# Moving adaLN sums between stages and reordering the splits behind three boundaries in a two-layer fp32 trunk

## The chip, the cores and the metric

The kernel runs on one core of one Trainium2 chip. The metric is the device time of one execution in microseconds (us), as the median of the timed runs. Five engines of the core matter here: TensorE (PE, matmuls and transposes; PEld is its loading of weights, which overlaps), VectorE (DVE), ScalarE (ACT), GpSimd (POOL) and SyncE (SP). Each works through its own queue of instructions in order and waits on semaphores for the others. In this kernel SP's queue issues nearly all loads, POOL's queue issues a few loads and on-chip moves.

## The reference

Two layers over 512 tokens of width 1024, in fp32. Layer 0 mixes tokens by stick-breaking attention with 16 heads, layer 1 by a gMLP. Each mixer is followed by a SwiGLU of inner width 2816. Every sub-layer has a norm ahead of it and one behind it, and shift, scale and gate are computed from a vector c ("adaLN").

```python
def reference(x, c, ...):
    for i in range(DEPTH):
        shift, scale, gate = ada_modulation(c, mix_ada_w[i], mix_ada_b[i])
        h = rms_norm(x, mix_pre_g[i]) * (1.0 + scale) + shift
        if i % N_MIXERS == 0:
            y = stick_breaking_mixer(h, sb_w_qkv[j], sb_w_o[j])
        else:
            y = token_mixing_mixer(h, ...)
        x = x + gate * rms_norm(y, mix_post_g[i])
        shift, scale, gate = ada_modulation(c, ffn_ada_w[i], ffn_ada_b[i])
        h = rms_norm(x, ffn_pre_g[i]) * (1.0 + scale) + shift
        y = swiglu(h, ffn_w_gate[i], ffn_w_up[i], ffn_w_down[i])
        x = x + gate * rms_norm(y, ffn_post_g[i])
    return x
```

`ada_modulation` is `silu(c) @ w + b` with w of 1024 x 3072: 4 of these in all, 12 parts of 1024 x 1024 that have to be read and summed.

## The kernel before

**Tiling.** The 512 tokens are 4 tiles of 128 (tt = 0 to 3, in reversed order). Between stages the hidden state h stands transposed, as hT. TensorE multiplies in fp32r, and full precision comes from three products of high and low parts: `split` (L107) makes the high part by a copy on ScalarE and the low part by a subtraction on DVE, `mm3` (L99) issues high x high, high x low and low x high. So each weight, each hT and each activation costs one ScalarE and one DVE instruction. In rows of the profile the ends h and l tell the parts (wh, wl, hTh, hTl, Sh, Sl).

**Who orders the work.** Where `pe["chain"]` and the `chain` of the recorders `dve` and `act` (class `Written`, L55) are on, instructions run in the order of the program text; `order` (L80) adds a dependency that orders only and waits for nothing. Where the chains are off (v's stage, the boundaries, the FFNs and the gMLP) a scheduler places the instructions of each engine.

**Stages.** In the profiled execution v's stage runs to about 92 us, attention to 231, its output projection and first boundary to 280, the first FFN to 606, the boundary behind it to 638, the gMLP to 766, its boundary to 793, and the second FFN to the end.

**adaLN in the background.** `Bg` (L310) computes parts of the modulation (G a gate, A a scale, B a shift) in small steps. A step is one load of 512 KB (`rawada`, two buffers, the next load issued when one is free; in attention on POOL's queue) and one DVE `scalar_tensor_tensor` that adds it to an accumulator; eight steps make a part. Then the accumulator is split (`acch`, `accl`), and two matmuls against a matrix of ones sum it over the partitions (bank `adaps`). `bg.step(n)` is called wherever the code places it.

**v's stage and attention.** While q, k of pair 0 and the first half of v exist, the loop of L941 to L950 multiplies the second half of v over 8 k-blocks, and takes one adaLN step in each of the first six (L949). `evac_q` (L755) makes q on ScalarE and `qlow` on DVE, out of the bank `pqk`, and thus frees that bank; `evac_k` (L768) does it for k. Then 8 pairs of heads follow (L961). Each pair has seven places where `rest()` takes matmuls of the next pair's q and k (`FILLS`, L809) and adaLN steps (`SUMS`, L812, one row a pair). `scores` (L859) makes sigmoids `ga` on ScalarE and a scan over them on DVE. `v_next` (L827) makes V's differences along the tokens, for which it moves V by one row with five moves on POOL's queue, into two buffers, and `step_v` subtracts; the first half's is made at L936, the second's behind pair 0, with the subtractions behind pairs 1 and 2 (L983 to L986).

**Boundaries.** `out_proj` (L484) ends the mixers and the first FFN, and `boundary` (L407) goes with each tile: two squares and a root give the norm of y, then x is updated (x<-t,r,x), t is x times A, divided by x's own norm, plus B (t<-t,r,B), and TensorE transposes t in two banks (`tp`, L438), which `split` turns into hT. Tiles 0 and 1 keep copies `c`. Behind the boundaries of tiles 2 and 3, `sums` (L452) makes the four sums S that the block products need, split too. Boundaries 0 and 1 stand between matmuls of the projection. Ahead of those of tiles 2 and 3 a unit of the next stage is put (`nxt[0]`, `nxt[1]`, L548), which reads tiles 0 and 1 alone, and a third one behind (`nxt[2]`, L551). For the FFNs these are `Ffn.first` (L1038): units on bank `gu` over the first 256 tokens, with their weights made by `wget` two units ahead (`look`); for the gMLP `u_first` (L1284), on bank `u`.

**The FFN's blocks.** After three units over the other 256 tokens the FFN goes on in `seven` (L1041): a product of 2x2 blocks by seven products in place of eight (bank `r`), the third of which is the first to read a sum S. `blocks` (L168) prepares its weights from two loads, `rawx` and `rawy`: split of x, split `b21` (named b in the profile), the addition `f13` and two more (named f), and their splits.

**Weights.** `wemit` (L132) takes a weight from one of two raw buffers and splits it, in the order of the list `stream`. The look-ahead decides how early its split is issued.

Of the kernel before, what the change touches and what calls it, by code (L numbers as in the profile page):

```python
# [25 lines left out]
def trunk(ctx: ExitStack, tc: tile.TileContext, A: dict, out: bass.AP):  # L26
# [28 lines left out]
    class Written:  # L55

        def __init__(self, engine):
            self.engine, self.prev, self.chain = engine, None, False

        def __getattr__(self, name):  # L60
            f = getattr(self.engine, name)

            def call(*a, **k):
                b = f(*a, **k)  # L64
                if self.chain and self.prev is not None:
                    order(b, self.prev)
                self.prev = b
                return b

            return call  # L70
# [97 lines left out]
    def blocks(xr, yr):  # L168

        fp = fwork["pool"]  # L170
        x = wtile(KD, P)
        split(x[0][:], x[1][:], xr[:])
        b21 = [fp.tile([P, 4, P], F32R, tag=f"b21{i}", name=nm("b21")) for i in range(2)]
        split(b21[0][:], b21[1][:], yr[:, 0:4, :])
        f13 = fp.tile([P, KD, P], F32, tag="f13", name=nm("f13"))
        dve.tensor_tensor(
            f13[:].rearrange("p (a k) f -> p a (k f)", a=2),
            xr[:].rearrange("p (a k) f -> p a (k f)", a=2),
            yr[:, 4:8, :].rearrange("p (a k) f -> p a (k f)", a=1).to_broadcast([P, 2, 512]),
            ALU.add,  # L180
        )
        t13 = wtile(KD, P)
        split(t13[0][:], t13[1][:], f13[:])
        f24 = fp.tile([P, KD, P], F32, tag="f24", bufs=1, name=nm("f24"))
        dve.tensor_tensor(f24[:, 0:4, :], f13[:, 0:4, :], xr[:, 4:8, :], ALU.add)
        dve.tensor_tensor(f24[:, 4:8, :], f24[:, 0:4, :], yr[:, 0:4, :], ALU.add)
        t24 = wtile(KD, P)
        split(t24[0][:], t24[1][:], f24[:])

        def half(t, i):  # L190
            return lambda k: (t[0][:, 4 * i + k, :], t[1][:, 4 * i + k, :])

        return {
            "B11": half(x, 0), "B22": half(x, 1), "B21": half(b21, 0),
            "T1": half(t13, 0), "T3": half(t13, 1), "T2": half(t24, 0), "T4": half(t24, 1),
        }
# [210 lines left out]
    def boundary(s, tt, y, xin, hT, S, tag):  # L407

        halves = [slice(0, 512), slice(512, D)]
        sq = [small.tile([P, 1], F32, tag=f"sq{hf}", name=nm("sq")) for hf in range(2)]  # L410
        t = npool.tile([P, D], F32, tag="n", name=nm("t"))
        for hf, c in enumerate(halves):
            act.activation(junk[:, c], y[hf][:], AF.Square, accum_out=sq[hf][:])
            if hf == 1:
                sd, r2 = rms(sq[1][:], sq[0][:])
            dve.tensor_tensor(t[:, c], y[hf][:], ada["G", s][:, c], ALU.mult)
        dve.reciprocal(r2[:], sd[:])
        x = xin(tt)
        if s == 3:
            for c in halves:  # L420
                dve.scalar_tensor_tensor(x[:, c], t[:, c], r2[:, 0:1], x[:, c], ALU.mult, ALU.add)
                load(out[tt * P : (tt + 1) * P, c], x[:, c])
            return
        dve.scalar_tensor_tensor(x[:], t[:], r2[:, 0:1], x[:], ALU.mult, ALU.add)
        xd[tt] = dram.tile([P, D], F32, tag=f"x{tt}", bufs=2, name=nm("xd"))
        nc.gpsimd.dma_start(out=xd[tt][:], in_=x)
        sx = small.tile([P, 1], F32, tag="sx", name=nm("sx"))
        act.activation(junk[:], x[:], AF.Square, accum_out=sx[:])
        sd, r1 = rms(sx[:])
        dve.tensor_tensor(t[:], x[:], ada["A", s], ALU.mult)  # L430
        dve.reciprocal(r1[:], sd[:])
        dve.scalar_tensor_tensor(t[:], t[:], r1[:, 0:1], ada["B", s], ALU.mult, ALU.add)
        late = []
        for q in range(2):
            ps = bank("tp", tag)
            for k in range(4):
                kk = q * 4 + k
                transpose(ps[:, k * P : (k + 1) * P], t[:, kk * P : (kk + 1) * P])  # L438
            a = ps[:].rearrange("p (a b) -> p a b", a=4)
            if tt % 2 == 0:  # L440
                hT[tt // 2, q] = (slot(F32R, "hTh", 4, 256), slot(F32R, "hTl", 4, 256))
            c = slice(tt % 2 * P, (tt % 2 + 1) * P)
            th, tl = hT[tt // 2, q]
            split(th[:, :, c], tl[:, :, c], a)
            if S is not None and tt < 2:
                if tt == 0:
                    S["c", q] = slot(F32, "c", 4, 256)
                act.activation(S["c", q][:, :, tt * P : (tt + 1) * P], a, AF.Copy)
            late.append(a)
        return lambda: sums(S, tt, late)  # L450

    def sums(S, tt, a):  # L452

# [19 lines left out]
        part("3", f[:, 0])  # L473

    xd = {}

    def x_load(tt):

# [5 lines left out]
    def out_proj(s, nk, get_act, wkey, J, bg, hT, nxt=(), pre=None, S=None, steps=0, bg2=None):  # L484
# [61 lines left out]
        for n, tt in enumerate((2, 3)):  # L546
            if nxt:
                evacs.append(nxt[n]())  # L548
            late.append(boundary(s, tt, y[tt], xin, hT, S, "p" if tt == 3 else "b"))
        if nxt:  # L550
            evacs.append(nxt[2]())  # L551
            with tc.issue_after(last_sqrt[0].ins):
                for f in evacs:
                    f()
        if hT is not None:
            for f in late:
                f()

    def sqrt_table():
        with tc.issue_after(last_act[0].ins):  # L560
# [185 lines left out]
    with tc.tile_pool(name="att", bufs=1) as att, tc.tile_pool(name="att2", bufs=6) as att2:  # L746
# [62 lines left out]
        FILLS = ((2, 3, 2, 3, 2, 3, 1),) * 5 + (  # L809
            (2, 2, 2, 2, 2, 2, 0), (4, 2, 1, 1, 0, 0, 0), (3, 0, 2, 0, 2, 1, 0),  # L810
        )
        SUMS = ((1, 0, 1, 0, 1, 0, 0),) * 6 + ((1, 1, 1, 1, 1, 1, 0), (1, 0, 1, 0, 1, 1, 0))  # L812
        fgen = filler()

        def fill(n):
# [125 lines left out]
        for k in range(KD):  # L941
            if k % 2 == 0:
                wv = wget(("wv", 1, k // 2))
            v_step(vb, 1, k, wv)
            if k in (1, 4):
                cur[0](B31 if k == 1 else B2)
            if k >= 6:
                step_v(k - 6)
            if k < 6:  # L949
                bg.step(1)  # L950
        v_evac(vb, 1)
        tw = [bank("tw") for _ in range(2)]
# [8 lines left out]
        for i in range(NPAIR):  # L961
            scores, flip, values, finish = cur
            more = i + 1 < NPAIR
            if more:
                cur = attend(i + 1)
            F = iter(zip(FILLS[i], SUMS[i]))

            def rest():
                n, sums = next(F)
                fill(n)  # L970
                bg.step(sums)

            for group, js in zip((LATE, *EARLY), (B31, B2, B0)):
                flip(group, 0)
                flip(group, 1)
                rest()
                if more:
                    cur[0](js)
                rest()
            values()  # L980
            finish()
            rest()
            if i == 0:  # L983
                step_v = v_next(1)
            if i in (1, 2):
                step_v(i - 1)  # L986
        for _ in fgen:
            bg.step(1)
        bg.step(99)
# [16 lines left out]
    class Ffn:  # L1006
# [29 lines left out]
            return evac  # L1036

        def first(self):  # L1038
            return [lambda f=f: self.unit(f, 0, 256, 2) for f in range(NH)]

        def seven(self, f):  # L1041

# [456 lines left out]
```

## Time and profile before

| | us |
|---|---|
| median of 3 runs | 1132.68 (1132.51 to 1133.71) |
| the profiled execution | 1135.05 |
| its span on the core | 1133.3 |
| DVE busy | 893.4 (79%) |
| ScalarE busy | 597.7 (53%) |
| loading of weights into TensorE | 993.3 (88%) |
| mean DMA traffic | 155 GB/s |

The span is the stretch from the first to the last instruction in the trace, the execution's time has what lies around it too. A share of busy time is an average over stages that have different limits, so what a wait costs is read from the stage in which it stands. TensorE's granted clock is at 0.9 or more of full speed in every fortieth of the span.

In rows of the timeline the columns are: start in us, duration in us, engine, line, operation, output<-inputs, partitions x elements and type, and the number of instructions (x2: two of them in one row, with their joint duration); in brackets the idle time of that engine just before, and what ended it.

### The profile page before, as it was taken

What the parts mean: (1) busy time and instruction counts of PE and PEld (TensorE: products, weight loads), DVE (VectorE), ACT (ScalarE), POOL (GpSimd) and SP (SyncE); (2) the same over time, 40 slices, a digit from 0 to 9 for tenths busy, and PEclk for the clock granted to TensorE, in tenths of its full rate; (3) what the DMA queues carried; (4) which work ended last, traced back from release to release, by engine and by line L of the source; (5) the groups of instructions that cost most, each with busy time, mean ns of one, the idle gap of its engine ahead of it and who ended that gap; (6) DMA issues with size and microseconds to landing.
All of it is one profiled execution on the core that took longest, in us unless ns stands there. A gap on an engine that the chain in (4) does not pass through costs nothing.

```text
span 1133.3 us, 18148 instructions
## 1 busy us (share of the span) xinstructions
PE 1110.5 (98%) x7264; PEld 993.3 (88%) x7264; DVE 893.4 (79%) x1141; ACT 597.7 (53%) x971; POOL 39.8 (4%) x71
## 2 busy tenths in 40 slices
PE   7999999999999999999999999999999999999997
PEld 5787878778999999988878978988999999999895
DVE  7767988759988989687677765659988888788964
ACT  7745666646555555562334534437455555566541
POOL 0212010000000000010000000000000000000000
PEclk9999999999999999999999999999999999999999
DMA  9676444353244444378874572333244344223242
GB/s 363 224 221 186 149 149 132 129 186 132 92 131 150 143 134 133 95 229 262 286 262 151 195 268 83 106 130 131 84 140 140 124 134 144 75 78 109 93 167 75
DMA packets 51298, 176.09 MB, mean 155 GB/s; under 512 B 5643, under 2 KB 6155, under 8 KB 50318
## 3 DMA queue, kind: packets, MB, share of 16 engines
q1 hardware_dynamic: 45166, 153.95, 41.2%
q0 software_dynamic: 6048, 20.98, 6.0%
q8 instruction: 57, 0.93, 0.3%
q14 instruction: 27, 0.22, 0.1%
HBM read 164.43 MB, written 8.39 MB: 152 GB/s over the span
## 4 chain that ended last, share of the span: by engine, by line
PE 74%; DMA 12%; DVE 9%; issue 2%; ACT 2%; SPq 0%; DVEq 0%; ACTq 0%
PE r L88 32%; PE y L88 10%; PE X L88 8%; DMA rawada<-in_ada 6%; PE pqk L88 6%; PE gu L88 4%; PE v L88 3%; PE M L88 2%; DVE wl L64 2%; PE u L88 2%; PE z L88 2%; PE tw L96 1%; PE av L88 1%; DMA raw<-in_wdown 1%; DMA ada<-in_ada0w 1%
## 5 line engine op out<-in xcount | busy, mean ns | idle before, releaser
L64 ACT ACTIVATE wh<-raw 128x1024 fp32r<-128x1024 f32 (+1 forms) x112 | 117.1, 1051 | 142.1 <-PE y L88 36.3
L64 DVE TENSOR_TENSOR wl<-raw,wh 128x1024 fp32r<-128x1024 f32 (+1 forms) x112 | 135.1, 1211 | 63.4 <-ACT wh L64 62.9
L88 PE MATMUL r<-Sh,wh 128*128 128x256 f32 x608 | 170.6, 281 | 0.0
L88 PE MATMUL r<-Sl,wh 128*128 128x256 f32 x608 | 170.5, 280 | 0.0
L88 PE MATMUL r<-Sh,wl 128*128 128x256 f32 x608 | 170.3, 280 | 0.0
L88 PE MATMUL y<-wh,as 128*128 128x512 f32 x480 | 153.6, 396 | 0.6 <-DVE G L64 0.6
L64 DVE TENSOR_TENSOR wl<-f,wh 128x1024 fp32r<-128x1024 f32 x76 | 92.9, 1222 | 37.1 <-ACT wh L64 37.0
L64 ACT ACTIVATE wh<-f 128x1024 fp32r<-128x1024 f32 x76 | 80.6, 1061 | 75.1 <-PE r L88 65.1
L88 PEld LDWEIGHTS r<-Sh,wh 128*128 128x128 f32 x608 | 114.8, 189 | 0.2 <-ACT e L64 0.2
L88 PEld LDWEIGHTS r<-Sh,wl 128*128 128x128 f32 x608 | 114.8, 189 | 0.0
L88 PEld LDWEIGHTS r<-Sl,wh 128*128 128x128 f32 x608 | 114.7, 189 | 0.0
L88 PEld LDWEIGHTS y<-wh,as 128*128 128x128 f32 x480 | 90.1, 188 | 21.6 <-DVE G L64 1.1
L88 PE MATMUL y<-wl,as 128*128 128x512 f32 x240 | 94.7, 395 | 0.0
L88 PE MATMUL r<-hTh,wh 128*128 128x256 f32 x304 | 88.9, 293 | 0.1
L88 PE MATMUL r<-hTl,wh 128*128 128x256 f32 x304 | 85.1, 280 | 0.0
L88 PE MATMUL X<-wh,as 128*128 128x512 f32 (+1 forms) x288 | 84.7, 370 | 0.0
L88 PE MATMUL r<-hTh,wl 128*128 128x256 f32 x304 | 80.3, 280 | 0.0
L64 ACT ACTIVATE e<-r 128x256 f32<-128x256 f32 x114 | 43.5, 381 | 53.6 <-PE r L88 53.3
L88 PEld LDWEIGHTS r<-hTh,wh 128*128 128x128 f32 x304 | 57.2, 188 | 4.8 <-DVE gu L64 1.3
L88 PEld LDWEIGHTS X<-wh,as 128*128 128x128 f32 x288 | 52.5, 188 | 9.6
L88 PE MATMUL r<-hTh,b 128*128 128x256 f32 x304 | 60.8, 282 | 0.0
L64 ACT ACTIVATE wh<-rawx 128x1024 fp32r<-128x1024 f32 x38 | 40.3, 1061 | 34.0 <-PE r L88 31.0
(233 smaller groups left out, 2812.9 us busy)
## 6 DMA issues: line engine op xcount, KB each, us to landing
rawada<-in_ada SPq DMA_DIRECT2D x56, 512.0 KB, 4.7
raw<-in_wdown SPq DMA_DIRECT2D x44, 512.0 KB, 4.0
rawy<-in_wy SPq DMA_DIRECT2D x38, 512.0 KB, 3.6
rawx<-in_wx SPq DMA_DIRECT2D x38, 512.0 KB, 4.3
rawada<-in_ada POOLq DMA_DIRECT2D x24, 512.0 KB, 4.3
raw<-in_wqk SPq DMA_DIRECT2D x16, 512.0 KB, 4.2
ada<-in_ada0w SPq DMA_DIRECT2D x7, 1026.0 KB, 11.0
raw<-in_wgu SPq DMA_DIRECT2D x12, 512.0 KB, 3.6
```

Of the source, the lines that this page charges most:

```text
L64: b = f(*a, **k)
L88: b = nc.tensor.matmul(o, l, r, start=start, stop=stop, skip_group_check=True)
L96: last_tp[0] = nc.tensor.transpose(o, i, ident)
```

## The change

It has three parts.

1. **Boundaries.** `Written` gets a `gate`: while it is set, each recorded instruction is ordered behind that one. `boundary` no longer splits tile 2's transposes; that code is now the function `turned`, and `out_proj` calls it for tile 2 behind the boundary of tile 3, with DVE gated by tile 3's t (`ready[0]`) and ScalarE by its last root. The third unit, with its two weights and whatever its look-ahead makes, is called inside the gates too. The addition `f13` of every block is ordered behind `ready[0]`, and `first` gives the second unit no look-ahead, so that the third unit's weights are made where it stands itself.
2. **Sums.** v's stage takes four adaLN steps instead of six, and pairs five and six of attention take four each instead of three.
3. **V's second moves** are written behind pair 1 instead of pair 0, and their subtractions behind pairs 2 and 3.

```diff
@@ class Written @@
-            self.engine, self.prev, self.chain = engine, None, False
+            self.engine, self.prev, self.chain, self.gate = engine, None, False, None
...
+                if self.gate is not None:
+                    order(b, self.gate)
@@ def blocks @@
-        dve.tensor_tensor(
+        add = dve.tensor_tensor(
             f13[:].rearrange("p (a k) f -> p a (k f)", a=2),
...
+        order(add, ready[0])
@@ def boundary @@
-        dve.scalar_tensor_tensor(t[:], t[:], r1[:, 0:1], ada["B", s], ALU.mult, ALU.add)
+        ready[0] = dve.scalar_tensor_tensor(t[:], t[:], r1[:, 0:1], ada["B", s], ALU.mult, ALU.add)
...
-            a = ps[:].rearrange("p (a b) -> p a b", a=4)
-            if tt % 2 == 0:
+            late.append(ps[:].rearrange("p (a b) -> p a b", a=4))
+        if tt != 2:
+            turned(tt, hT, S, late)
+        return lambda: sums(S, tt, late), lambda: turned(tt, hT, S, late)
+
+    def turned(tt, hT, S, late):
+
+        for q, a in enumerate(late):
+            if (tt // 2, q) not in hT:
                 hT[tt // 2, q] = (slot(F32R, "hTh", 4, 256), slot(F32R, "hTl", 4, 256))
...
-            late.append(a)
-        return lambda: sums(S, tt, late)
...
+    ready = [None]
@@ def out_proj @@
         if nxt:
+            dve.gate, act.gate = ready[0], last_sqrt[0]
+            late[0][1]()
             evacs.append(nxt[2]())
+            dve.gate = act.gate = None
...
-                f()
+                f[0]()
@@ attention @@
-        SUMS = ((1, 0, 1, 0, 1, 0, 0),) * 6 + ((1, 1, 1, 1, 1, 1, 0), (1, 0, 1, 0, 1, 1, 0))
+        SUMS = ((1, 0, 1, 0, 1, 0, 0),) * 4 + ((1, 1, 1, 0, 1, 0, 0),) * 2 + ((1, 1, 1, 1, 1, 1, 0), (1, 0, 1, 0, 1, 1, 0))
...
-            if k < 6:
+            if k < 4:
                 bg.step(1)
...
-            if i == 0:
+            if i == 1:
                 step_v = v_next(1)
-            if i in (1, 2):
-                step_v(i - 1)
+            if i in (2, 3):
+                step_v(i - 2)
@@ Ffn.first @@
-            return [lambda f=f: self.unit(f, 0, 256, 2) for f in range(NH)]
+            return [lambda f=f: self.unit(f, 0, 256, 2 if f != 1 else 0) for f in range(NH)]
```

Numbers behind names in the rows below count tiles and differ between the two kernels. DVE's queue at the end of v's stage before (G<-rawada is an adaLN sum, wl a weight's low part, ga the scans, qlow what frees the bank pqk):

```order
L64 SCALAR_TENSOR_TENSOR G_568<-rawada_622,sc,G_568 128x1024
L64 SCALAR_TENSOR_TENSOR G_568<-rawada_637,sc,G_568 128x1024
L64 SCALAR_TENSOR_TENSOR G_568<-rawada_667,sc,G_568 128x1024
L64 TENSOR_TENSOR wl_731<-raw_726,wh_730 128x1024
L64 SCALAR_TENSOR_TENSOR ga_756<-ga_756,tri 128x512 x2
L64 SCALAR_TENSOR_TENSOR qlow<-pqk_725,q_767 64x512 x2
```

The same place in the changed kernel:

```order
L64 SCALAR_TENSOR_TENSOR G_568<-rawada_622,sc,G_568 128x1024
L64 TENSOR_TENSOR wl_725<-raw_720,wh_724 128x1024
L64 SCALAR_TENSOR_TENSOR ga_750<-ga_750,tri 128x512 x2
L64 SCALAR_TENSOR_TENSOR qlow<-pqk_719,q_761 64x512 x2
L64 TENSOR_TENSOR wl_772<-raw_722,wh_771 128x1024
```

Two sums no longer stand ahead of wl, the scans and qlow. DVE's queue in the second half of the sixth pair, before:

```order
L64 SCALAR_TENSOR_TENSOR qlow<-pqk_1616,q_1688 64x512 x2
L64 TENSOR_TENSOR wl_1709<-raw_1617,wh_1708 128x1024
L64 SCALAR_TENSOR_TENSOR B_1396<-rawada_1666,sc,B_1396 128x1024
L64 SCALAR_TENSOR_TENSOR ga_1725<-ga_1725,tri 128x256 x2
L64 SCALAR_TENSOR_TENSOR B_1396<-rawada_1718,sc,B_1396 128x1024
L64 SCALAR_TENSOR_TENSOR ga_1759<-ga_1759,tri 128x512 x2
L64 TENSOR_TENSOR k_1770<-pqk_1705,k_1770 64x512 x2
```

In the changed kernel:

```order
L64 SCALAR_TENSOR_TENSOR qlow<-pqk_1613,q_1685 64x512 x2
L64 SCALAR_TENSOR_TENSOR B_1496<-rawada_1663,sc,B_1496 128x1024
L64 TENSOR_TENSOR wl_1709<-raw_1614,wh_1708 128x1024
L64 SCALAR_TENSOR_TENSOR B_1496<-rawada_1692,sc,B_1496 128x1024
L64 SCALAR_TENSOR_TENSOR ga_1725<-ga_1725,tri 128x256 x2
L64 SCALAR_TENSOR_TENSOR B_1496<-rawada_1718,sc,B_1496 128x1024
L64 SCALAR_TENSOR_TENSOR ga_1759<-ga_1759,tri 128x512 x2
L64 TENSOR_TENSOR k_1770<-pqk_1705,k_1770 64x512 x2
```

One sum more stands there, between qlow and wl, and it works through its own load. DVE's queue at the boundary of tile 3 behind attention, before (t_2474 is tile 3's, hTl_2399 and hTl_2408 from tp_2393 and tp_2402 are tile 2's low parts, the two wl are the third unit's weights, f the blocks' additions):

```order
L64 SCALAR_TENSOR_TENSOR x_2258<-t_2474,r_2482,x_2258 128x1024
L64 TENSOR_TENSOR wl_2414<-raw_2411,wh_2413 128x1024
L64 TENSOR_TENSOR wl_2420<-raw_2417,wh_2419 128x1024
L64 TENSOR_TENSOR hTl_2399<-tp_2393,hTh_2398 128x4x128
L64 TENSOR_TENSOR hTl_2408<-tp_2402,hTh_2407 128x4x128
L64 TENSOR_TENSOR t_2474<-x_2258,A_944 128x1024
L64 RECIPROCAL r_2492<-sd_2490 128x1
L64 TENSOR_TENSOR f_427_2526<-rawx_2510,rawy_2511 128x1024
L64 SCALAR_TENSOR_TENSOR t_2474<-t_2474,r_2492,B_1396 128x1024
```

In the changed kernel (tile 3's t is t_2454; tile 2's banks are tp_2393 and tp_2398, tile 3's tp_2476 and tp_2481; b are the low parts of b21):

```order
L64 SCALAR_TENSOR_TENSOR x_2258<-t_2454,r_2462,x_2258 128x1024
L64 TENSOR_TENSOR t_2454<-x_2258,A_1055 128x1024
L64 RECIPROCAL r_2472<-sd_2470 128x1
L64 SCALAR_TENSOR_TENSOR t_2454<-t_2454,r_2472,B_1496 128x1024
L64 TENSOR_TENSOR wl_2501<-raw_2498,wh_2500 128x1024
L64 TENSOR_TENSOR wl_2507<-raw_2504,wh_2506 128x1024
L64 TENSOR_TENSOR b_426_2523<-rawy_2511,b_425_2522 128x512
L64 TENSOR_TENSOR b_438_2548<-rawy_2515,b_437_2547 128x512
L64 TENSOR_TENSOR hTl_2487<-tp_2393,hTh_2486 128x4x128
L64 TENSOR_TENSOR hTl_2487<-tp_2476,hTh_2486 128x4x128
L64 TENSOR_TENSOR hTl_2491<-tp_2481,hTh_2490 128x4x128
L64 TENSOR_TENSOR hTl_2491<-tp_2398,hTh_2490 128x4x128
```

Both steps of t now follow x at once; the weights' low parts, the two b and tile 2's low parts stand behind them. On TensorE the third unit's first six matmuls, which stood ahead of tile 3's transposes, now stand behind them.

## The prediction

> **What bounds the kernel now.** I read the page's busy table first, then TensorE's waits, then the timeline around each of them. The busy table:
>
> ```profile
> PE 1110.5 (98%) x7264; PEld 993.3 (88%) x7264; DVE 893.4 (79%) x1141; ACT 597.7 (53%) x971; POOL 39.8 (4%) x71
> ```
>
> TensorE is busy for 98% of the span of 1133.3 us, and the change leaves the number of its matmuls as it was. So it can only win where TensorE stands still, and only lose by a new standstill. The view of waits of TensorE (engine, output and line, what it waited for: us in total, times, the longest) has these among its rows:
>
> ```profile
> PE pqk L88 <- DVE qlow L64: 2.5, 1, 2.5
> PE tp L96 <- DVE t L64: 1.9, 3, 0.8
> ...
> PE adaps L88 <- DVE accl L64: 0.8, 2, 0.6
> PE adaps L88 <- ACT acch L64: 0.8, 2, 0.6
> PE y L88 <- DVE k L64: 0.7, 1, 0.7
> ```
>
> Row one is the end of v's stage, row two the transposes of tile 3 at the three boundaries, the last the end of the sixth pair. The real price is a little above these figures, as the timeline shows (start in us, duration, instruction, in brackets the idle time before it and what ended it):
>
> ```profile
> 88.47 0.39 PE L88 MATMUL pqk<-hTl,wh 128*128 128x512 f32 x1
> 88.70 0.40 PE L88 MATMUL pqk<-hTh,wl 128*128 128x512 f32 x1
> 91.58 0.47 PE L88 MATMUL pqk<-hTh,wh 128*128 128x512 f32 x1 [2.48 <-DVE qlow L64]
> ```
>
> From the second to the third it is 2.88 us, start to start; the undisturbed step, from the first to the second, is 0.23. So 2.65 us are lost, 0.17 more than the bracket says, because a matmul's shown end overlaps the next one's start. I add 0.16 to every bracket below.
>
> **The sums leave v's stage.** DVE works its queue in order. Up to the wait it does this (G<-rawada are the adaLN sums):
>
> ```profile
> 79.12 1.28 DVE L64 SCALAR_TENSOR_TENSOR G<-rawada,sc,G 128x1024 f32<-128x1024 f32 x1 [0.20 <-DMA rawada<-in_ada]
> 82.72 1.29 DVE L64 SCALAR_TENSOR_TENSOR G<-rawada,sc,G 128x1024 f32<-128x1024 f32 x1 [2.32 <-DMA rawada<-in_ada]
> 85.34 1.28 DVE L64 SCALAR_TENSOR_TENSOR G<-rawada,sc,G 128x1024 f32<-128x1024 f32 x1 [1.33 <-DMA rawada<-in_ada]
> 86.54 1.22 DVE L64 TENSOR_TENSOR wl<-raw,wh 128x1024 fp32r<-128x1024 f32 x1
> 87.68 2.33 DVE L64 TENSOR_TENSOR_SCAN ga<-ga,tri 128x512 f32<-128x512 f32 x2
> 90.04 1.39 DVE L64 SCALAR_TENSOR_TENSOR qlow<-pqk,q 64x512 fp32r<-64x512 f32 x2
> ```
>
> The sums at 82.72 and 85.34 are the two that go. They cost 2.57 us of work and 3.65 us of waiting for loads, 6.2 us in all, and wl, the scans and qlow queue behind them. Without them wl runs at 80.4 to 81.6. What is late next is ScalarE's q, which qlow needs:
>
> ```profile
> 83.51 1.21 ACT L64 ACTIVATE q<-pqk 64x512 fp32r<-64x512 f32 x2 [0.77 <-PE pqk L88]
> ```
>
> It is done at 84.7. The scans take 2.33 us and come after their sigmoids, so from about 82.3 to 84.7, and qlow runs from 84.8 to 86.2. TensorE wants the bank at 88.93. That is 2.7 us to spare, so the whole 2.65 us go: **-2.65**.
>
> The POOL queue changes with it. The two loads for these sums no longer stand ahead of V's second moves, so these five moves are issued from about 81 us rather than 85, although the program text calls for them a pair later. The subtractions they feed (1.2 us each on DVE) move to the ends of pairs three and four; the values that read them come at the end of pair five, over 10 us later. I cost both at nothing. The loads of the weights run beside the moves before and after.
>
> **The sums arrive in pairs five and six.** The fifth pair has room for its new one: it fills DVE's idle time there. In the sixth pair the rows of before are
>
> ```profile
> 192.76 1.39 DVE L64 SCALAR_TENSOR_TENSOR qlow<-pqk,q 64x512 fp32r<-64x512 f32 x2 [0.24 <-ACT q L64]
> 195.96 1.23 DVE L64 TENSOR_TENSOR wl<-raw,wh 128x1024 fp32r<-128x1024 f32 x1 [1.81 <-ACT wh L64]
> ...
> 199.48 1.26 DVE L64 SCALAR_TENSOR_TENSOR B<-rawada,sc,B 128x1024 f32<-128x1024 f32 x1
> 200.66 2.34 DVE L64 TENSOR_TENSOR_SCAN ga<-ga,tri 128x512 f32<-128x512 f32 x2
> 203.01 1.39 DVE L64 TENSOR_TENSOR k<-pqk,k 64x512 fp32r<-64x512 f32 x2
> ```
>
> The new sum falls into the 1.81 us ahead of wl, at 194.15 to 195.43, and costs nothing itself. But two buffers serve all the loads, so the last sum's load (due at 199.48) can only be issued when the new sum has freed its buffer. In before it was freed five microseconds earlier. The page's DMA row gives the price:
>
> ```profile
> rawada<-in_ada POOLq DMA_DIRECT2D x24, 512.0 KB, 4.3
> ```
>
> 4.3 us is the median to landing, and those of these pairs took about 4. With 0.4 us from the freed buffer to the issue the data are there at about 199.9: the sum, the two scans and k come 0.45 us later, and k is what TensorE already waits for (0.7 us in the last row of the waits). **+0.45**. The lower end is 0 (a load in 3.6 us), the upper 1.0 (one in 4.9); a gain here is excluded, since only work is added ahead of k.
>
> [...]
>
> **The three boundaries.** At the first one DVE and TensorE do this:
>
> ```profile
> 269.29 1.28 DVE L64 SCALAR_TENSOR_TENSOR x<-t,r,x 128x1024 f32<-128x1024 f32 x1
> 271.18 2.48 DVE L64 TENSOR_TENSOR wl<-raw,wh 128x1024 fp32r<-128x1024 f32 x2 [0.61 <-ACT wh L64]
> ...
> 275.05 1.22 DVE L64 TENSOR_TENSOR t<-x,A 128x1024 f32<-128x1024 f32 x1
> ...
> 277.37 1.28 DVE L64 SCALAR_TENSOR_TENSOR t<-t,r,B 128x1024 f32<-128x1024 f32 x1
> ```
> ```profile
> 278.71 0.66 PE L96 MATMUL tp<-pack,t 128*128 128x128 f32 x4 [0.81 <-DVE t L64]
> ```
>
> Tile 3's x is ready at 270.57, but t only at 278.65: two weight splits, tile 2's two splits and one f13 addition stand in between. In the new order t follows x: 270.6 to 271.8 for the product, ScalarE's square and root until 272.1 beside it, the last step until 273.6. TensorE arrives at 277 (the six matmuls of the third unit that stood ahead of the transposes now follow them), so its wait is gone with 3 us to spare. The same holds at the other two. Together: 1.9 us of the waits row and three times 0.16, **-2.35** (-0.97, -0.43, -0.94).
>
> What comes later instead: the weight splits (until 276.0; their matmuls start behind the transposes at 277.8), and tile 2's splits (tile 3's and 2's low parts until 280.5 by walking the new queue; asked for from 283.4). The b splits of the first two blocks, done in an idle stretch in before, now stand in this queue too, 2 x 0.69 us. How full DVE is shows the view by stages (stretch, its length, busy time and count of PE, PEld, DVE, ACT, POOL, then clock and DMA):
>
> ```profile
> 262.00:302.00 40.00, 39.19 (x321) 38.42 (x320) 38.77 (x53) 23.22 (x40) 2.03 (x3) 1.00 0.38 124
> ```
>
> DVE has 1.2 us free in 40. So its backlog lasts to the first block product that reads the sums S, which begins 24 matmuls after r starts, at 303.3 in the new order. Walking the new queue with the durations of before, the first S is complete at 298.8; 4.5 us remain. At the gMLP boundary the first unit of the second half waits for the last of the four late splits (tile 2's second):
>
> ```profile
> 637.98 1.09 ACT L64 ACTIVATE hTh<-tp 128x512 fp32r<-128x512 f32 x2 [0.66 <-PE tp L96]
> ```
>
> 0.55 us each on ScalarE, three of them behind the transposes, then one low part on DVE: ready at 640.0, asked for at 640.5. That is the thinnest cover, and if it fails TensorE pays the lateness itself, some tenths.
>
> **A side effect in the gMLP stage.** The b splits of the second FFN's first two blocks leave ScalarE's queue there:
>
> ```profile
> 674.29 0.63 ACT L64 ACTIVATE b<-rawy 128x512 fp32r<-128x512 f32 x1 [6.65 <-DMA rawy<-in_wy]
> ...
> 677.22 0.63 ACT L64 ACTIVATE b<-rawy 128x512 fp32r<-128x512 f32 x1 [1.35 <-DMA rawy<-in_wy]
> 677.76 0.61 ACT L64 ACTIVATE acch<-A 128x512 fp32r<-128x512 f32 x1
> ```
> ```profile
> 678.42 0.50 PE L88 MATMUL adaps<-acch,ones 128*128 128x512 f32 x1 [0.21 <-ACT acch L64]
> 679.15 0.50 PE L88 MATMUL adaps<-accl,ones 128*128 128x512 f32 x1 [0.23 <-DVE accl L64]
> ```
>
> Each b waited for its block's load with the rest of ScalarE's queue behind it. Without them acch can go at about 675.5, and accl on DVE at 676.5, over a microsecond before TensorE comes. By starts (the matmul before began at 677.82; usual step 0.23) the two waits cost 0.37 and 0.50: **-0.87**. The ends are -0.87 and 0, the latter if acch and accl are then held up by something else in their queues; I take the full value, since ScalarE stood idle for 6.65 us ahead of the first b. One SP load of a weight also moves ahead of a rawada load in this stage; that load comes under a microsecond later and its sum is due 3 us before the splits.
>
> **Sum.** -2.65 + 0.45 - 2.35 - 0.87 = -5.4 us, on a profiled execution of 1135.05 us (span 1133.3 and 1.75 around it): 1129.6. The runs' median was 1132.68, so 2.4 us below the profiled one; I forecast **1127.3** for the median.
>
> **The rivals.**
> - *Attention takes part of it back.* DVE gets 2.57 us of sums in pairs five and six, and the sixth pair ends in a wait for DVE. If both sums come fully onto the path to k, the loss is 2.57 instead of 0.45: -3.3, 1129.4. For it: TensorE waits for k already. Against: the 1.81 us of idle time into which one goes. 12%.
> - *The boundaries give nothing.* The deferred splits become the new wait: the 2.35 us return at the next user (the third unit's weights, or the gMLP unit with 0.5 us of cover). -3.1, 1129.6. For: DVE is full there. Against: the margins of 1.8 to 4.5 us at the FFN boundaries. 12%.
> - *Slower: DVE's backlog reaches the block products.* At the first and third boundary the sums S are completed later than before (296.3 then, 298.8 by my count). Each microsecond beyond the margin of 4.5 us is paid twice, once per FFN boundary. To lose more than the gain of 5.4 us, S has to be 4.5 + 2.7 = 7.2 us later than I count; at 8 us late the time is 1134.3. For: DVE's 38.77 of 40 us. Against: the work added is 1.4 us of b. 4%.
> - *The change does not do what it says.* The sums leave but qlow still waits, for its q or a scan, and t stays late: 1132.7. Against: the orders on DVE are as the change says. 3%. (V's moves do not in fact come later, as shown; that costs nothing.)
>
> **How the numbers follow.** My forecast has 69%, its own range -4.0 to -5.9 us (the pair at 0 to 1.0, the side effect at 0 to -0.87), so 1126.8 to 1128.7, with some 0.7 more at the lower end for the spread of the runs (1132.51 to 1133.71 before). To leave out no more than 2 in 10 the range reaches over the first two rivals: 1126.1 to 1129.9. About 0.2%, or 2.3 us, is what a measurement of this kernel can tell from no change: faster than 1130.4 is the forecast and most of both rivals, 0.88; the same 0.08; slower 0.04.
>
> **What would show it.** Right: no idle time ahead of the pqk matmul near 89 us, and TensorE's wait for k near 202 us at about 1.2 us; no wait of tp for t; adaps near 675 without waits. Wrong: waits of gu, u or r for hTl, wl or Sl behind the boundaries, a wait for k above 2 us, or the load of the last B sum landing late by more than a microsecond.

## The result, and the profile after

The changed kernel takes 1129.13 us (median of 15 runs, 1127.59 to 1132.01), the kernel before in the same series 1133.71 us (15 runs, 1130.88 to 1138.72). The ratio is 0.9961, with a 95% interval from 0.9949 to 0.9973, or -4.4 us (-5.8 to -3.1). The forecast was -5.4 us and 1127.3. The profiled execution is 1129.13 us, its span 1127.4, which is 5.9 us below the span of the profile before.

The busy table of the profile after shows the same number of matmuls and the same DVE time. The span is 5.9 us shorter: TensorE's standstill fell by 3.1 us and its shown busy time by 2.8. A part of each wait stands in that busy time (0.17 us at the wait of 2.48, by the starts), which explains some of the 2.8:

```profile
PE 1107.7 (98%) x7264; PEld 993.5 (88%) x7264; DVE 893.6 (79%) x1141; ACT 599.0 (53%) x971; POOL 39.7 (4%) x71
```

The view of TensorE's waits after (what it waited for: us in total, times, longest), without the rows of the program's start:

```profile
PE adaps L90 <- ACT acch L64: 2.2, 1, 2.2
PE y L90 <- DVE k L64: 1.7, 1, 1.7
...
PE y L90 <- DVE G L64: 0.2, 1, 0.2
```

pqk for qlow and tp for t have left the table. The wait for k has grown from 0.7 to 1.7. The wait for acch is not the old one of the gMLP: it stands in the first FFN's down projection, where before had two short ones (0.56 each in brackets, for acch and for accl).

DVE's timeline at the end of v's stage:

```profile
77.74 1.26 DVE L64 SCALAR_TENSOR_TENSOR G<-rawada,sc,G 128x1024 f32<-128x1024 f32 x1
79.18 1.23 DVE L64 TENSOR_TENSOR wl<-raw,wh 128x1024 fp32r<-128x1024 f32 x1 [0.18 <-ACT wh L64]
82.13 2.34 DVE L64 TENSOR_TENSOR_SCAN ga<-ga,tri 128x512 f32<-128x512 f32 x2 [1.73 <-ACT ga L64]
84.60 1.39 DVE L64 SCALAR_TENSOR_TENSOR qlow<-pqk,q 64x512 fp32r<-64x512 f32 x2
```

qlow ends at 86.0; TensorE wants the bank near 88.9 and does not stop. At the boundary behind attention DVE, and TensorE's transposes:

```profile
267.44 1.28 DVE L64 SCALAR_TENSOR_TENSOR x<-t,r,x 128x1024 f32<-128x1024 f32 x1
268.76 1.22 DVE L64 TENSOR_TENSOR t<-x,A 128x1024 f32<-128x1024 f32 x1
270.27 0.16 DVE L64 RECIPROCAL r<-sd 128x1 f32<-128x1 f32 x1 [0.29 <-ACT sd L64]
270.47 1.29 DVE L64 SCALAR_TENSOR_TENSOR t<-t,r,B 128x1024 f32<-128x1024 f32 x1
```
```profile
275.18 1.04 PE L98 MATMUL tp<-pack,t 128*128 128x128 f32 x8
```

t is ready at 271.76, 3.4 us ahead of the transposes, which carry no bracket. The sixth pair, where the time went up:

```profile
190.48 1.36 DVE L64 SCALAR_TENSOR_TENSOR qlow<-pqk,q 64x512 fp32r<-64x512 f32 x2
191.87 1.28 DVE L64 SCALAR_TENSOR_TENSOR B<-rawada,sc,B 128x1024 f32<-128x1024 f32 x1
193.10 1.22 DVE L64 TENSOR_TENSOR wl<-raw,wh 128x1024 fp32r<-128x1024 f32 x1
194.25 1.28 DVE L64 SCALAR_TENSOR_TENSOR B<-rawada,sc,B 128x1024 f32<-128x1024 f32 x1
...
197.61 1.28 DVE L64 SCALAR_TENSOR_TENSOR B<-rawada,sc,B 128x1024 f32<-128x1024 f32 x1 [0.90 <-DMA rawada<-in_ada]
198.81 2.33 DVE L64 TENSOR_TENSOR_SCAN ga<-ga,tri 128x512 f32<-128x512 f32 x2
201.16 1.39 DVE L64 TENSOR_TENSOR k<-pqk,k 64x512 fp32r<-64x512 f32 x2
```

DVE now stands idle for 0.90 us for the load of the last B sum, and scans and k come behind it. TensorE's wait at the end:

```profile
202.70 0.47 PE L90 MATMUL y<-wh,o 128*128 128x512 f32 x1 [1.73 <-DVE k L64]
```

### The profile page after: what moved, and what is told of

The parts are those of the page before. It is cut to its first block, busy times and chain, and to the rows that moved or that the text cites. A ratio compares the mean times of both kernels' runs of the same rounds, so it can differ in the third digit from the quotient of the medians.

```text
span 1127.4 us, 18149 instructions
## 1 busy us (share of the span) xinstructions
PE 1107.7 (98%) x7264; PEld 993.5 (88%) x7264; DVE 893.6 (79%) x1141; ACT 599.0 (53%) x971; POOL 39.7 (4%) x71
## 4 chain that ended last, share of the span: by engine, by line
PE 84%; DMA 7%; DVE 5%; issue 2%; ACT 1%; SPq 0%; POOL 0%; DVEq 0%; POOLq 0%; ACTq 0%
PE r L90 33%; PE y L90 12%; PE X L90 8%; PE v L90 7%; PE gu L90 6%; DMA rawada<-in_ada 5%; PE pqk L90 5%; PE u L90 4%; PE M L90 2%; PE z L90 1%; PE tw L98 1%; PE av L90 1%; DMA ada<-in_ada0w 1%; PE tp L98 1%; DMA raw<-in_wdown 1%
## 5 line engine op out<-in xcount | busy, mean ns | idle before, releaser
L90 PE MATMUL r<-hTh,wh 128*128 128x256 f32 x304 | 88.9, 293 | 0.0
```

The lines of the kernel that those rows point to most:

```text
L90: b = nc.tensor.matmul(o, l, r, start=start, stop=stop, skip_group_check=True)
```

## The experiments

Twelve experiments were run; ratios are against the kernel before, with 95% intervals. "Loss" is the start-to-start time of two matmuls less their usual step, as in the prediction.

**The kernel before, a second execution (r1_before).** No edit.

> The kernel before once more, as one look at how its waits differ from execution to execution. If the wait of pqk for qlow and that of adaps for acch near 568 us hang on when loads land, they come out at other lengths than 2.65 and 1.4 us (1.3 to 2.6 and 1.4 to 3.3 by the profiles of kernels that share these places), while the wait of y for k (0.88) and those of tp for t that hang on DVE's queue alone repeat within 0.1 to 0.5 us. If all repeat, the differences between the profiles are the edits'.

TensorE at the end of v's stage in this execution:

```profile
88.25 0.40 PE L88 MATMUL pqk<-hTh,wl 128*128 128x512 f32 x1
89.58 0.47 PE L88 MATMUL pqk<-hTh,wh 128*128 128x512 f32 x1 [0.94 <-DVE qlow L64]
```

The loss is 1.10 us where the first profile had 2.65, in the same program. The wait for acch near 568 us costs 2.59; the first profile had 0.71 there and 0.73 for accl five microseconds later, 1.43 together. The wait for k repeats at 0.88, the three waits for t come to 1.18, 0.62 and 0.71 (0.97, 0.43 and 0.94 in the first profile). So the two that follow a chain of loads differ by 1.55 and 1.16 us between these two executions. The chain of the adaLN loads in v's stage shows it on POOL's queue, where DMA_DIRECT2D rows are issues, in the first profile and then in this one:

```profile
72.06 0.56 POOL L105 DMA_DIRECT2D rawada<-in_ada  x1 [5.04 <-DVE G L64]
```
```profile
70.18 0.56 POOL L105 DMA_DIRECT2D rawada<-in_ada  x1 [5.17 <-DVE G L64]
```

The first profile's chain is 1.9 us later here and qlow at its end 2.0 us (90.04 against 88.05), while TensorE wants the bank only 0.45 us later (88.93 against 88.48).

**The sums alone (e1_sums).**

```diff
-        SUMS = ((1, 0, 1, 0, 1, 0, 0),) * 6 + ((1, 1, 1, 1, 1, 1, 0), (1, 0, 1, 0, 1, 1, 0))
+        SUMS = ((1, 0, 1, 0, 1, 0, 0),) * 4 + ((1, 1, 1, 0, 1, 0, 0),) * 2 + ((1, 1, 1, 1, 1, 1, 0), (1, 0, 1, 0, 1, 1, 0))
-            if k < 6:
+            if k < 4:
```

> Only the sums are moved (four steps in v's stage, one more in pairs five and six); boundaries and V's moves stay as before. Theory (the terms add): TensorE's wait for qlow near 89 us goes (-2.65), the wait at the end of pair six grows from 0.88 to about 1.9 (+1.0), nothing else moves: -1.65 us against before. The wait ahead of adaps near 566 us, 1.4 us in before and 2.4 in the changed kernel, stays at 1.4 if the reordered boundaries cause it, and grows if the sums do. Rival (the sums are only delayed, all their work comes back at the end of pair six): +2.6 there, 0.0 us in all.

Ratio 0.9994 (0.9981 to 1.0006), 12 runs: -0.7 us (-2.2 to +0.7). The wait for qlow is gone, that for k costs 2.12 (0.88 before), not the +2.6 of the rival. With a v's-stage wait of 1.1 to 2.65 this part is worth between nothing and -1.4; the interval holds both the theory and zero. The wait near 568 us costs 2.19, and the boundaries are as before here. In this profile TensorE's granted clock is 0.53 from 204.0 to 207.5 us, behind the wait for k: from the first matmul behind the wait to the y behind the next z are 4.90 us (202.78 to 207.68), where the changed kernel takes 3.33 for the same matmuls (202.70 to 206.03), so 1.6 us less. The timed runs point the same way: their mean clock is 0.9956, that of the 26 runs of the kernel before beside them 0.9970, an estimated 0.8 us by the line in the last section. That the longer wait for k causes this is likely and not shown.

**The boundaries alone (e2_bound).** The changed kernel with the sums and V's moves of before (the second and third part of the diff undone).

> Only the boundaries are reordered; sums and V's moves stay as before. Theory: the three waits of tp for t go (-2.35), the two adaps waits in the gMLP go (-0.87 to -1.1), 2.5 us at pqk and 0.9 at pair six stay: -3.2 to -3.5 us against before. Rival (a boundary's gain comes back at its next user): -0.9 or less, with a new wait of gu, u or r for hTl, wl or Sl behind the boundary.

Ratio 0.9964 (0.9948 to 0.9980), 9 runs: -4.1 us (-5.9 to -2.3). No wait of tp for t, none of adaps in the gMLP, and no new wait of gu, u, r for hTl, wl or Sl behind a boundary. Nearly all of the change's gain is here. The wait near 566 us costs 3.33, the longest of all profiles; pqk loses 1.73.

**V's second moves alone (e3_moves).**

```diff
-            if i == 0:
+            if i == 1:
                 step_v = v_next(1)
-            if i in (1, 2):
-                step_v(i - 1)
+            if i in (2, 3):
+                step_v(i - 2)
```

> Only V's second moves and their subtractions come a pair later. Theory: 0.0 us (within 0.3), since the values that read them come at the end of pair five; the waits of before stay as they are. Rival (the moves crowd the weights' loads in the first pair, or the two later subtractions push k in pairs three and four): a gain or a loss of 0.5 us or more, with a wait of pqk, tw or y in pairs one to four.

Ratio 0.9999 (0.9985 to 1.0014), 12 runs: nothing that can be told. No wait in pairs one to four is new; pqk loses 1.30 here, with the old sums.

**Tile 2's splits back in place (e7_inplace).** Out of the changed kernel:

```diff
-        if tt != 2:
-            turned(tt, hT, S, late)
+        turned(tt, hT, S, late)
...
-            late[0][1]()
```

> The changed kernel, but tile 2's transposes are split at their old place, ahead of tile 3's last step; the gates of the third unit and of f13 stay. Theory: what delayed t at the two FFN boundaries was mostly the third unit's weights (2.3 us) and f13 (1.1 us); tile 2's two low parts (1.3 us) push t from 3.5 us ahead of the transposes to about 2 us ahead, so no wait of tp for t comes back: 0.0 us against the changed kernel, -4.4 against before. Rival (the deferral of tile 2's splits is what brings the gain): a wait of tp for t of 0.4 to 1 us at each boundary, +1 to +2.4 us against the changed kernel.

Ratio 0.9978 (0.9967 to 0.9988), 12 runs: -2.5 us (-3.7 to -1.4), whose interval overlaps that of the change (-5.8 to -3.1). No wait of tp for t comes back at any of the three boundaries: t is ready 2.2, 1.3 and 2.2 us before its transposes (at the first, at 274.04 for 276.24). So the gates of the third unit and of f13 are enough for the waits that went. The profile has one new loss in their place, 0.54 us in the second FFN's first block, where r waits for gu on DVE:

```profile
819.55 0.39 PE L90 MATMUL r<-hTh,wh 128*128 128x256 f32 x1 [0.37 <-DVE gu L64]
```

The same row shows up in e8_bfree (0.41 loss) and not in the changed kernel. The wait for k has 2.43. These two come to 1.1 us (0.54, and 2.43 less 1.88), but the wait for acch near 568 us is 0.49 shorter than in the changed kernel, so the profile does not explain the 1.9 us between the two point values; the intervals allow nothing as well as all of it.

**b free of the gates (e8_bfree).** Out of the changed kernel, in `blocks`:

```diff
+        held, dve.gate, act.gate = (dve.gate, act.gate), None, None
         split(b21[0][:], b21[1][:], yr[:, 0:4, :])
+        dve.gate, act.gate = held
```

> The changed kernel, but the splits of b21 are free of the gates, so that they stand where the scheduler puts them, in the gMLP stage again around acch as before. Theory (the gMLP's adaps waits came from b's loads in ScalarE's queue): two waits of adaps near 675 us of 0.4 to 0.7 us each come back, +0.9 to +1.2 us against the changed kernel, and no wait comes back at the boundaries. Rival (the adaps waits went because the boundary ahead ended sooner): no wait of adaps there, 0.0 us.

Ratio 0.9990 (0.9979 to 1.0002), 12 runs: -1.1 us (-2.4 to +0.2). ScalarE's timeline in the gMLP stage shows b ahead of and behind acch again, each behind its load, and TensorE waits:

```profile
673.74 0.63 ACT L64 ACTIVATE b<-rawy 128x512 fp32r<-128x512 f32 x1 [2.98 <-DMA rawy<-in_wy]
674.28 0.61 ACT L64 ACTIVATE acch<-A 128x512 fp32r<-128x512 f32 x1
675.75 0.63 ACT L64 ACTIVATE b<-rawy 128x512 fp32r<-128x512 f32 x1 [0.85 <-DMA rawy<-in_wy]
```
```profile
676.35 0.49 PE L90 MATMUL adaps<-accl,ones 128*128 128x512 f32 x1 [0.39 <-DVE accl L64]
```

On DVE the first b's low part (674.41 to 675.10) stands ahead of accl, which runs from 675.62. Two losses of 0.55 and 0.45 are back, which the changed kernel has not, while the boundaries stay without a wait; so the gMLP's gain is from b. With the 0.41 for gu that is 1.4 of the 3.3 us by which this kernel stands behind the changed one, where 0.9 to 1.2 were expected. Another 1.5 us, an estimate from 3.00 us at a granted clock of 0.50 in place of 1.00, are no waits at all: the view by stretches (length, busy time and count of PE, PEld, DVE, ACT, POOL, then granted clock and DMA) shows for this kernel and then for the changed one, behind the long wait near 566 us (2.3 us here, 2.2 there),

```profile
569.50:572.50 3.00, 3.00 (x8) 2.34 (x8) 3.00 (x4) 1.04 (x2) 0.00 (x0) 0.50 0.74 220
```
```profile
569.50:572.50 3.00, 3.00 (x15) 2.33 (x14) 3.00 (x5) 1.13 (x2) 0.00 (x0) 1.00 0.76 208
```

8 matmuls in place of 15, at half the clock. Kernels without this edit have such stretches too (the last section), and of the two executions of the kernel before one has it and the other has not, so the edit is not needed for it. The 12 timed runs have a mean clock of 0.9961, the changed kernel's 15 runs 0.9973: an estimated 0.7 us of the 3.3 by the line in the last section.

**Pair six with two sums (e5_pair6two, r2_pair6two).** Out of the changed kernel:

```diff
-        SUMS = ((1, 0, 1, 0, 1, 0, 0),) * 4 + ((1, 1, 1, 0, 1, 0, 0),) * 2 + ((1, 1, 1, 1, 1, 1, 0), (1, 0, 1, 0, 1, 1, 0))
+        SUMS = ((1, 0, 1, 0, 1, 0, 0),) * 2 + ((1, 1, 1, 0, 1, 0, 0),) * 3 + ((1, 0, 1, 0, 0, 0, 0), (1, 1, 1, 1, 1, 1, 0), (1, 0, 1, 0, 1, 1, 0))
```

> The changed kernel, with the two sums and one more of pair six in pairs three to five (four steps each), so that pair six has two. Theory (the wait for k at the end of pair six is the chain last load, last sum, two scans, k on DVE): with that sum gone k comes at least 1.9 us earlier and the wait of 1.9 us goes, no other wait appears, since DVE stands idle for 1.7 us ahead of k in pairs three and four: -1.9 us against the changed kernel, -6.3 against before if the changed kernel is at -4.4. Rival (DVE is full in the attention as a whole, so the sums cost wherever they stand): a new wait of y, tw or pqk in pairs three to five of 0.5 us or more each, and less than 0.5 us gained.

> The kernel of e5_pair6two once more, beside e11_acch on one chip, to hold the two against each other. Theory: -6 to -8 us against before, no wait of y for k at the end of pair six again.

Ratio 0.9929 (0.9911 to 0.9947) with 6 runs, and 0.9956 (0.9940 to 0.9971) with 12 runs on another occasion: -8.1 and -5.0 us. The two intervals overlap between 0.9940 and 0.9947; the second run fell short of the -6 to -8 expected, which its interval (-6.8 to -3.3) touches. In both profiles the wait for k is gone and pairs three to five show no new one. The expected step of -1.9 from the change fits the profiles (1.88 to 0); the times hold it, but the second run alone (-5.0 against -4.4) could not tell it from nothing.

**Which part of the sixth pair's loss is what (e12_pair46, e4_pair45).** The added sums stand in pairs four and six, or in pairs four and five:

```diff
+        SUMS = ((1, 0, 1, 0, 1, 0, 0),) * 3 + ((1, 1, 1, 0, 1, 0, 0), (1, 0, 1, 0, 1, 0, 0)) + ((1, 1, 1, 0, 1, 0, 0), ...)
```
```diff
+        SUMS = ((1, 0, 1, 0, 1, 0, 0),) * 3 + ((1, 1, 1, 0, 1, 0, 0),) * 2 + ((1, 0, 1, 0, 1, 0, 0), ...)
```

> The changed kernel, with the added sum of pair five in pair four instead. Theory (the +1.0 at the end of pair six has two parts: 0.45 to 0.5 that the last load comes after its buffer, and 0.5 that pair five's sums run late and push the first half of pair six's queue): the new sum of pair six starts about 0.5 us earlier within the pair and the wait of y for k is 1.3 to 1.5 us instead of 1.9 to 2.4. Rival (all of it is the load in pair six): 1.9 to 2.4 us.

> The changed kernel, with the added sums in pairs four and five, none in pair six. Theory of two parts: the last load is no longer late, and what pair five pushes is the 0.5 us: the wait of y for k is 0.9 to 1.4 us. Rival (all of it is pair six's own fourth load): 0.88 us, as in before.

One execution each. In e4_pair45 the loss at k is 1.19: 0.31 more than before, with no sum added in pair six itself. So what pair five pushes is a part of its own. In e12_pair46 the new sum starts at 191.22, 0.65 earlier than in the changed kernel (0.55 counted from where TensorE wants k), as expected. But the loss is 2.41, outside the expectation, because the last load takes longer:

```profile
192.91 0.53 POOL L107 DMA_DIRECT2D rawada<-in_ada  x1 [4.70 <-DVE B L64]
```
```profile
198.03 1.28 DVE L64 SCALAR_TENSOR_TENSOR B<-rawada,sc,B 128x1024 f32<-128x1024 f32 x1 [1.43 <-DMA rawada<-in_ada]
```

From issue to the sum are 5.1 us here. In the changed kernel the same load was issued at 193.56 and its sum began at 197.61, 4.05 us later; in e1_sums, e8_bfree and e7_inplace it took 4.7, 4.4 and 4.9. Counted from where TensorE wants k, these five loads were issued 7.25 us (the changed kernel) to 7.80 us (e12_pair46) ahead, and their sums began 3.20 to 2.66 us ahead, the load issued last having the earliest sum. So an earlier issue did not bring an earlier sum here; what held the loads up is not shown.

**Two tries at the wait in the first FFN (e9_order, e11_acch).** It is in all profiles, so it is not the change's, but it is the longest left. The first orders one weight split behind the second acch (`bg.high` holds these instructions), the second also what follows on ScalarE until the end of the projection, each on the kernel of e5_pair6two:

```diff
+            if mid is not None and k == mid + 2:
+                act.gate = bg.high[1]
             w = pre["w"][k] if k < npre else wget(wkey(k))
+            act.gate = None
```
```diff
+            if mid is not None and k == mid + 2:
+                act.gate = bg.high[1]
...
+        act.gate = None
         sqrt_table()
```

> The kernel of e5_pair6two, and in the first FFN's down projection the weight split that waits for its load is ordered behind the second acch of A on ScalarE. Theory (acch is ready at 562.4 in e5_pair6two and waits only because that split, whose load lands between 1.4 and 3.3 us late in the six profiles so far, stands ahead of it): the wait of adaps near 564 us goes, -1.4 to -3.3 us against the kernel of e5_pair6two, about -9.5 against before. Rival (the weight is what TensorE needs next): the wait moves to y<-wh behind it, 0.0 us.

> The kernel of e5_pair6two, and on ScalarE in the first FFN's down projection the splits of the later activations are ordered behind the second acch of A too, not the weight split alone. Theory (in e9_order acch stood behind eight such splits of 0.5 us, which themselves began late behind a load): acch runs after three of them, at about 562.3, and the wait of adaps of 1.4 to 3.3 us shrinks below 0.5: -1 to -2.5 us against the kernel of e5_pair6two. Rival (the split that begins late behind its load sets everything that follows): the wait stays at 1.4 us or more, 0.0 us.

e9_order: ratio 0.9949 (0.9930 to 0.9967). The wait stayed, at 2.36: the expectation fell. ScalarE shows why:

```profile
558.77 1.06 ACT L64 ACTIVATE wh<-raw 128x1024 fp32r<-128x1024 f32 x1 [5.53 <-DMA raw<-in_wdown]
559.74 1.07 ACT L64 ACTIVATE yp<-y 128x512 f32<-128x512 f32 x2
560.69 4.26 ACT L64 ACTIVATE as<-act 128x512 fp32r<-128x512 f32 x8
564.85 0.62 ACT L64 ACTIVATE acch<-A 128x512 fp32r<-128x512 f32 x1
```

An earlier weight split begins late behind its load, and eight splits of activations stand between it and acch. e11_acch moves five of them behind: ratio 0.9938 (0.9925 to 0.9952), 6 runs, -7.0 us (-8.5 to -5.4), beside r2_pair6two's -5.0 on the same chip. The wait of 2.12 us that r2_pair6two has falls to 0.60 for acch and 0.56 for accl, 1.16 in all and not below the 0.5 expected, and a loss of 0.87 for y<-G that r2_pair6two has is not there:

```profile
561.12 1.67 ACT L64 ACTIVATE as<-act 128x512 fp32r<-128x512 f32 x3
562.68 0.62 ACT L64 ACTIVATE acch<-A 128x512 fp32r<-128x512 f32 x1
```

Both beat the kernel before. In the same series the median of e11_acch is 1125.69 us (1125.25 to 1127.17), that of r2_pair6two 1127.93 (1124.92 to 1132.26), though their ratios' intervals overlap between 0.9940 and 0.9952. The lowest ratio of all is e5_pair6two's 0.9929, in another series, so which of the two kernels is faster is not settled.

## Why the prediction came out as it did

The direction was right and the time lies in the range; the gain was some 1 us smaller than forecast. The gain of 4.4 us lies in the forecast's own range of 4.0 to 5.9. The time of 1129.13 us does not lie in its own 1126.8 to 1128.7, but in the part that was added for the rivals, because the kernel before stood at 1133.71 in the common series and not at 1132.68. The time alone is as near to the first two rivals (1129.4 and 1129.6) as to that range; what tells them apart is the waits. Term by term, with the losses in the profile before, in that of the changed kernel, and their means. The old state of each place has four profiles (before twice, and two of e1_sums, e2_bound and e3_moves), the new sixth pair four as well (the changed kernel, e1_sums, e7_inplace, e8_bfree):

| term | forecast | the two profiles | by the means |
|---|---|---|---|
| sums leave v's stage | -2.65 | 2.65 to 0 | 1.70 to 0: -1.7 |
| the sixth pair | +0.45 | 0.88 to 1.88: +1.0 | 0.88 to 2.10: +1.2 |
| three boundaries | -2.35 | 2.34 to 0 | 2.31 to 0: -2.3 |
| gMLP's adaps (the means with a third loss of 0.25, see below) | -0.87 | 0.87 to 0 | 1.3 to 0: -1.3 |
| sum | -5.4 | | -4.1 |

The two spans differ by 5.9 us. The two profiles' terms come to -4.9; with the third loss (-0.25), the losses near 566 and 574 us (+0.92) and that of y for G (-0.37) it is -4.6, and for the other 1.3 us no single place was found.

- **v's stage: mechanism right, size off.** qlow was forecast to end at 86.2 and ends at 86.0, with the scans behind their sigmoids as the limit. But "2.65 us are lost" was one execution's value of a wait that hangs on a chain of loads: 2.65, 1.10, 1.73 and 1.30 in the four profiles that have it. The forecast's own range took two ends for the sixth pair and for the side effect, and none for this term, the largest of the sum.
- **The sixth pair: mis-sized, and its first step was wrong.** The load part held in the changed kernel: freed buffer, 0.4 us to the issue (193.15 to 193.56), four microseconds to landing. But "the fifth pair has room for its new one" did not hold. Its last sum waits 1.29 us for its load in the changed kernel, the row below, and scan, wl and the next pair's first sum come later, so that pair six's new sum starts 0.5 us later within the pair than forecast; e4_pair45 shows this push alone at 0.31. The load part was then sized by one value, 4.1 us, where the runs show 4.05 to 5.1. The upper end given, 1.0, was exceeded in four of five profiles (1.24, 1.10 and 1.55 more than before in e1_sums, e8_bfree and e7_inplace, 1.53 in e12_pair46). A wait for k above 2 us and a last load late by more than a microsecond were named as signs of being wrong; the changed kernel's profile shows neither (a loss of 1.88, and DVE idle for 0.90 us for the load), but e1_sums and e7_inplace, with the same sixth pair, show both (2.12 and 1.14, 2.43 and 1.44).

```profile
181.74 1.29 DVE L64 SCALAR_TENSOR_TENSOR B<-rawada,sc,B 128x1024 f32<-128x1024 f32 x1 [1.29 <-DMA rawada<-in_ada]
```

- **The boundaries: right in place and size.** All three waits went, and in the changed kernel nothing took their place (e7_inplace and e8_bfree have a wait of r for gu near 820 us). The thinnest cover held too: the last of the gMLP's low parts was forecast 0.5 us ahead of its user, and is ready at 637.25 for a unit that begins near 637.7. What the working did not see is that the deferral of tile 2's splits was not needed for that (e7_inplace).
- **The side effect in the gMLP: right**, shown by e8_bfree in both directions, and a third loss of 0.23 to 0.27 on the next pair of adaps, left out of the sum, went with it.
- **V's moves: right**, nothing in e3_moves.
- **Not in the working at all:** the losses near 566 and 574 us, which I counted as unaffected without asking how far they repeat. In the two profiles they go from 1.43 to 2.36. Nothing ties that to the change: 2.59 in the second execution of before, and 1.25 to 3.33 over the twelve profiles with the old order of that place.

The rivals: attention did take back more than forecast, by about a third of the way to that rival (+2.57). The boundaries' rival, the slower one and "no effect" did not occur: no wait for wl, hTl or Sl stands behind a boundary.

## What to carry to other kernels

A wait that ends with DVE but stands behind a chain of loads had no one length here (2.65, 1.10, 1.73 and 1.30 us at the end of v's stage): read the same place in two or three executions before its whole length goes into a sum, and give the range the spread. Look at the granted clock behind a long standstill of TensorE too: it was 0.50 for 3 us behind 2.42 us in r1_before, and 1.00 behind 2.20 us in the changed kernel. When work is moved to an engine's idle time, ask first what ended that idle time's neighbours; where two buffers feed it, the new step can delay the next load (the last one of the sixth pair was issued 7.25 us ahead of where TensorE wants k, 13.4 us before), and the lateness can travel into the following stage (0.31 us from pair five to pair six in e4_pair45). And where an order is written for one place, see which instructions go along with it (b and the gMLP here); these side effects can be a quarter of the gain.

## What the runs showed of the hardware

**Four standstills of TensorE cost more than their length.** Behind the wait for acch in r1_before, of 2.42 us, the steps of matmuls of 512 columns are 0.43 us in place of 0.23 for some 3 us, and the view by stretches has the granted clock there and ahead of it:

```profile
560.00:566.00 6.00, 6.00 (x26) 4.43 (x24) 4.26 (x5) 3.20 (x6) 0.00 (x0) 1.00 0.84 264
566.00:570.00 4.00, 1.58 (x7) 0.88 (x6) 4.00 (x8) 4.00 (x8) 0.00 (x0) 0.97 0.94 335
570.00:573.00 3.00, 3.00 (x7) 2.42 (x8) 2.62 (x3) 1.60 (x3) 0.00 (x0) 0.50 0.77 255
```

Six of these steps take 2.55 us (570.58 to 573.13), an estimated 1.2 us more than at 0.23. In e1_sums the clock is 0.53 from 204.0 to 207.5 us, behind the wait of 1.97 us for k, which cost 1.6 us by the starts given with that experiment. In e8_bfree it is 0.50 from 569.5 to 572.5 us, behind 2.3 us for acch, an estimated 1.5 us. In e2_bound, behind 3.2 us for acch, the clock is 0.78 and 0.70:

```profile
568.20:569.50 1.30, 0.00 (x0) 0.00 (x0) 0.57 (x2) 1.25 (x2) 0.00 (x0) 1.00 1.00 331
569.50:572.50 3.00, 2.62 (x9) 2.10 (x10) 3.00 (x4) 2.00 (x4) 0.00 (x0) 0.78 0.89 295
572.50:576.00 3.50, 3.50 (x13) 2.74 (x12) 2.27 (x4) 0.71 (x2) 0.00 (x0) 0.70 0.76 259
```

By the missing clock (3.00 us x 0.22 and 3.50 us x 0.30) that is an estimated 1.7 us. Two others went without: in the first profile of the kernel before the clock is 1.00 around the wait of 2.48 us for qlow, which ends at 91.58,

```profile
60.00:95.00 35.00, 32.52 (x144) 26.07 (x143) 24.80 (x24) 12.74 (x20) 6.31 (x12) 1.00 0.80 226
```

and in the changed kernel it is 1.00 from 564 to 576 us, around the wait of 2.20 us for acch. So these four cost more than the term that the wait itself shows, and the clock is one difference between the two executions of the kernel before. What decides whether it falls is not shown: the shortest of the four is 1.97 us long, and one of 2.48 us went without.

**The mean clock and the time.** Over the 170 runs of the study that list it, the granted clock lay between 0.992 and 0.999, and a straight line through time against clock, with a level for each kernel, has 0.57 us for each thousandth (standard error 0.09).

**Loads.** Of the five loads of 512 KB that feed the last sum of the sixth pair in as many kernels, and on which that sum waits, the shortest took 4.05 us from issue to sum and the longest 5.1.
